# A hybrid decoder layer on one core: part of the weight-splitting work of the recurrent stage goes to GpSimd, with the steps around it rearranged

## The chip, the cores and the metric

The kernel runs on one core of a Trainium2 chip. The metric is device time in microseconds for one execution. An execution is profiled by the hardware on top of the timed runs.

## What is computed

One inference step of one layer, for a prompt of 256 tokens and 8 sequences that decode one token each: 264 columns in all, model width 2048.

```
x = x + 0.5 * swiglu(rmsnorm(x, n1), f1g, f1u, f1d)      # d_ff 5504
proj = rmsnorm(x, nm) @ w_in                             # q, k, v and the RWKV columns
o_att  = sliding-window attention with sinks and relative bias (prompt and decode)
o_rwkv = RWKV-7 time mixing:  S = S*exp(lw) + (S @ -kk)(kk*a)^T + v k^T ;  y = S @ r
x = x + concat(o_att, o_rwkv) @ w_out
x = x + 0.5 * swiglu(rmsnorm(x, n2), f2g, f2u, f2d)
y = rmsnorm(x, final)
```

Beside y, the key and value windows, the recurrent state and the shift state are returned. In the time mixing, `kx = k * (1 + (a - 1) * ka)`.

## The kernel before, in words

Activations lie with features on the partitions and the 264 columns along the free dimension. All weights come from memory once, as chunks of up to 128 x 512 (four 128 x 128 blocks). A chunk is split in `chunk`: SyncE loads `raw`, ScalarE rounds it to `hi` (line 123), and `lo = raw - hi` is subtracted by the engine passed as `e` (through the helper `tt`, line 58). `gemm` multiplies each block three times: hi by the activations' upper part, hi by their lower part, lo by the upper part. There are 6 `raw` buffers and 4 each of `hi` and `lo`. In `gemm` the engine for `lo` is VectorE, always. The buffers are taken with high priority, so that chunks are prepared ahead.

The program has three stages. The first feed-forward ends at about 754 us, with the first chunk load of w_in. The recurrent stage (`mixing_body`) runs to about 1250 us, the second feed-forward to the end. Only the recurrent stage is edited.

In the recurrent stage the weight stream is w_in, 38 tiles of 4 chunks (`win`): two small tiles, then three tiles for each of 8 pairs of RWKV heads, then 4 key and value tiles, then 8 query tiles. w_out follows in three passes over its 16 outputs (`PASS`): pass 0 takes the mixed tiles 0 to 3 (one chunk an output), pass 1 the tiles 8 to 11, 4 and 5, pass 2 the tiles 6, 7 and 12 to 15 (each one full and one half chunk an output). Mixed tiles 0 to 7 are RWKV pairs, 8 to 15 attention tiles.

The rest of the stage is written as generators (tasks). After each chunk, `tick` gives every live task one turn. Tasks are:

- `prep`, one for each pair: decays, keys, the products for the chunked recurrence, and the copies of the 8 decode columns into `XD` by GpSimd.
- `chain`, one for each batch of two pairs (four batches, 0 to 3). It inverts unit triangular 32 x 32 blocks by forward substitution: 30 steps `s`, each a multiply into `st` and an add into `Xt` on VectorE, with a turn's end after every `NSTEP` steps. The result goes to memory (`sb<-Xt`) and comes back transposed over partitions (`TT<-sb`), with `DWAIT` turns of pause ahead of the substitution and behind the transfer; the identity is added to TT; then come VectorE transposes (`TN`), products on TensorE, copies into `W` and `uv`, a three-step scan over chunks, the group norm (`gnorm`, its reciprocal in line 677) and the gate product (`m<-sgl,ld`).
- `attend`, one for each query tile, and `dec_attend`, one for each four query tiles: scores, `softmax`, transposes, probabilities times V (for decode: `m<-uv,bk`), and for decode another transpose (line 818) and a copy into the query tile's last columns.

`drain` gives turns to the tasks whose results a pass needs before the pass is written; `split` then makes upper and lower parts of the mixed tiles, lower ones on GpSimd and VectorE in turn. The order of instructions within each engine is set when the program is built, by a scheduler that simulates times and follows the priorities. Each engine works its queue in order.

Of the kernel before, what the change touches and what calls it, by code (L numbers as in the profile page):

```python
# [9 lines left out]
AF = mybir.ActivationFunctionType  # L10
ALU = mybir.AluOpType
AX = mybir.AxisListType

P = 128
# [7 lines left out]
NPAIR = 8  # L22
NSH = 26
NIN = 38
HALF = (slice(0, 64), slice(64, 128))
# [4 lines left out]
NS, NO, NY, NH, NT, NLD = 38, 8, 8, 40, 18, 6  # L30
NWARM = 14
NGM, NKR, NUV, NTT, NBT = 10, 5, 3, 2, 5
NSTEP = 4
DWAIT = (8,8,8,4)
PW = (2, 1, 3, 2, 2)
ALPHA = math.exp(-0.5)
LKV = 26
# [5 lines left out]
VMU, VKK, VKA, VA0, VRK, VLW, VLB, VSK, VSD = 64, 90, 98, 106, 114, 122, 130, 138, 154  # L43
# [4 lines left out]
def body(tc, I, O):  # L48
    nc = tc.nc
    V, A, G, TE, SP = nc.vector, nc.scalar, nc.gpsimd, nc.tensor, nc.sync  # L50
# [6 lines left out]
    def tt(e, out, a, b, op):  # L57
        return e.tensor_tensor(out=out, in0=a, in1=b, op=op)  # L58
# [4 lines left out]
    def ts(e, out, a, s1, op0, s2=None, op1=None):  # L63
        k = {} if op1 is None else dict(op1=op1)
        e.tensor_scalar(out=out, in0=a, scalar1=s1, scalar2=s2, op0=op0, **k)

    def act(out, in_, f, **k):
        return A.activation(out=out, in_=in_, func=f, **k)  # L68

    def bc(ap, shape):  # L70
        return ap.broadcast_to(list(shape))
# [23 lines left out]
    with ExitStack() as ctx:  # L95
# [20 lines left out]
        def chunk(src, n, e, ahead=True):  # L116
            w = n * P
            with tc.high_priority() if ahead else nullcontext():
                raw = wp.tile([P, CH * P], F32, tag="raw", bufs=NRAW, name=uid("raw"))
                hi = wp.tile([P, CH * P], F32R, tag="hi", bufs=NHL, name=uid("hi"))  # L120
                lo = wp.tile([P, CH * P], F32R, tag="lo", bufs=NHL, name=uid("lo"))
                SP.dma_start(raw[:, :w], src)  # L122
                A.copy(hi[:, :w], raw[:, :w])  # L123
                tt(e, lo[:, :w], raw[:, :w], hi[:, :w].bitcast(F32), ALU.subtract)
            return hi, lo

        def gemm(ps, src, xs, step=None, rng=None, ahead=True):
            n = len(xs)
            for k0 in range(0, n, CH):
                k1 = min(n, k0 + CH)  # L130
                if rng and k0 not in rng:
                    continue
                hi, lo = chunk(src[:, k0 * P:k1 * P], k1 - k0, V, ahead)
                for k in range(k0, k1):
                    xh, xl = xs[k]
                    c = slice((k - k0) * P, (k - k0 + 1) * P)
                    mm(ps[:, :T], hi[:, c], xh, k == 0, False)
                    mm(ps[:, :T], hi[:, c], xl, False, False)
                    mm(ps[:, :T], lo[:, c], xh, False, k == n - 1)
                if step:  # L140
                    step()

        vec = cp.tile([P, NVEC], F32, name="vec")
# [13 lines left out]
        def vc(i):  # L157
            return vec[:, i:i + 1]
# [173 lines left out]
        def mixing_body(mx, n2, n3, XD):  # L332
            def fix(shape, name):
                return mx.tile(list(shape), F32, name=name)
# [9 lines left out]
            ident, bo, cm = C[:, CID:CID + P], C[:, CBO:CBO + P], C[:, CCM:CCM + P]  # L344
# [8 lines left out]
                G.memset(pj[:, 0:1], 0.0)  # L353
            nmu = fix((P, NSH), "nmu")
            mu = vec[:, VMU:VMU + NSH]
            ts(V, nmu, mu, -1.0, ALU.mult, 1.0, ALU.add)
            tt(V, ss, ss, bc(mu.unsqueeze(2), (P, NSH, NB)), ALU.mult)
            nbat = len(BATCH)
# [2 lines left out]
            mixed = [None] * 16  # L361
            have = [False]

            def win(t):
                ps = acc()
                gemm(ps, I["win"][t], n2.xs, tick)
                if not have[0]:
                    n2.rstd(rs)
                    have[0] = True
                return ps  # L370
# [20 lines left out]
            def prep(p, bt, k, xrr, xk, xv):  # L391
# [7 lines left out]
                sg, a = tmp(), tmp()  # L399
# [20 lines left out]
                rk = tmp((P, T + 2 * NB))  # L420
                stt(b, b, 1e24, kk, ALU.min, ALU.mult)
                tt(V, b, b, a, ALU.mult)
                ts(V, a, a, 1.0, ALU.subtract, vc(VKA + p), ALU.mult)
                kx = a
                stt(kx, a, 1.0, xk, ALU.add, ALU.mult)
                stt(rk[:, :T], xrr, vc(VRK + p), kx, ALU.mult, ALU.mult)
# [43 lines left out]
                for h in range(2):  # L470
# [3 lines left out]
                    for blk in range(2):  # L474
                        x = blk * 32
# [12 lines left out]
                for c in range(4):  # L488
                    for h in range(2):
                        r, o = HALF[h], HALF[1 - h]  # L490
# [24 lines left out]
            def chain(bt):  # L515
                n = bt.n
                while bt.left:
                    yield
                nr = n * 16
                ng = P // nr  # L520
                if ng == 3:
                    ng = 2
                nj = 32 // ng
                X = ring((ng * nr, 32, 32), "X", 1)
                Y = ring((ng * nr, nj, 32), "Xt", 1)
# [8 lines left out]
                for s in range(1, 31):  # L534
# [5 lines left out]
                    if s % NSTEP == 0:  # L540
                        yield
                for g in range(ng):
                    SP.dma_start(scr2[bt.i].rearrange("r (j g t) -> g r j t", g=ng, t=32)[g], Y[g * nr:(g + 1) * nr])
                yield from pause(1)
                for h in range(2):
# [2 lines left out]
                        SP.dma_start(TT[x:x + 32, :, blk * 32:blk * 32 + 32],  # L548
                                     scr2[bt.i].rearrange("(h b m) (s t) -> h b s m t", h=2, b=2, s=32)[h, blk])
                yield from pause(DWAIT[bt.i])  # L550
                for h in range(2):
                    for blk in range(2):
                        x = h * 64 + blk * 32
                        v = TT[x:x + 32, :, blk * 32:blk * 32 + 32]
                        tt(V, v, v, bc(ident[x:x + 32, x:x + 32].unsqueeze(1), (32, n * 4, 32)), ALU.add)
                TN = ring((P, n * 4, 32), "TN", 1)
                for h in range(2):
                    V.transpose(TN[h * 64:h * 64 + 32], TT[h * 64:h * 64 + 32, :, 0:32])
# [32 lines left out]
                for k in range(n):  # L591
                    v = wus[k].rearrange("p (c t) -> p c t", c=4)
                    A.copy(W[:, k], v[:, 1:4, 0:64])
                    for h in range(2):
                        V.tensor_copy(uv[HALF[h], :, k, HALF[h]], v[HALF[h], :, 64:128])  # L595
                yield
                pbs = [mp() for _ in range(n)]
                for k in range(n):
# [104 lines left out]
            def softmax(s, mxv, sinks, n):  # L703
                nm, sm, es = (ring((P, 2), "st" + x, 6) for x in "abc")
                ts(V, nm[:, :n], mxv[:, :n], -1.0, ALU.mult)
                for j in range(n):
                    act(s[j], s[j], AF.Exp, bias=nm[:, j:j + 1], accum_out=sm[:, j:j + 1])
                act(es[:, :n], nm[:, :n], AF.Exp, bias=sinks)
                tt(V, sm[:, :n], sm[:, :n], es[:, :n], ALU.add)
                V.reciprocal(sm[:, :n], sm[:, :n])  # L710
                for j in range(n):
                    ts(V, s[j], s[j], sm[:, j:j + 1], ALU.mult)

            def attend(t, q):
                p = t // 4
# [162 lines left out]
            for pi, ks in enumerate(PASS):  # L878
                now = need(ks)
                drain(now, [g for g in tasks if g not in now])  # L880
                with tc.high_priority():
                    for k in ks:
                        split(k)
                for o in range(KD):
                    ps = acc()
                    gemm(ps, I["wout"][o, :, k0 * P:(k0 + len(ks)) * P], [mixed[k] for k in ks], tick)
                    with tc.high_priority():
                        tt(V, xr[o], ps[:, :T], xr[o], ALU.add)
                    if pi == len(PASS) - 1 and o < CH:
                        n3.split(xr[o], tag="y")  # L890
                for k in ks:
                    mixed[k] = None
                k0 += len(ks)
# [148 lines left out]
```

## Time and profile before

| | |
|---|---|
| median of 3 runs | 2026.01 us (2024.55 to 2027.55) |
| profiled execution | 2027.84 us, its span 2026.1 us |
| mean granted TensorE clock | 0.994 |
| recurrent stage, about 770 to 1215 us | 445 us, VectorE busy 339 us, ScalarE 258 us, GpSimd 51 us |

In the rows, PE is TensorE's matmuls, PEld its weight loads, DVE VectorE, ACT ScalarE, POOL GpSimd, SP SyncE. A group's row has line, engine, operation, output<-inputs by the program's names, shapes, count, then busy us and mean ns of one, then idle time of the engine just ahead and what ended it. In the chain of waits, a row is start, length and what the end of the program depended on.

### The profile page before, as it was taken

What the parts mean: (1) busy time and instruction counts of PE and PEld (TensorE: products, weight loads), DVE (VectorE), ACT (ScalarE), POOL (GpSimd) and SP (SyncE); (2) the same over time, 40 slices, a digit from 0 to 9 for tenths busy, and PEclk for the clock granted to TensorE, in tenths of its full rate; (3) what the DMA queues carried; (4) which work ended last, traced back from release to release, by engine and by line L of the source; (5) the groups of instructions that cost most, each with busy time, mean ns of one, the idle gap of its engine ahead of it and who ended that gap; (6) DMA issues with size and microseconds to landing.
All of it is one profiled execution on the core that took longest, in us unless ns stands there. A gap on an engine that the chain in (4) does not pass through costs nothing.

```text
span 2026.1 us, 45592 instructions
## 1 busy us (share of the span) xinstructions
PE 1994.1 (98%) x17126; PEld 1956.0 (97%) x17126; DVE 1324.4 (65%) x2674; ACT 1041.4 (51%) x2054; POOL 240.8 (12%) x342
## 2 busy tenths in 40 slices
PE   9999999999999999999999899999999999999998
PEld 9999999999999999998888789999999999999998
DVE  5865555655556577678778766775666666566665
ACT  5644444444444466665454555554444444444445
POOL 0401001010110122111110000120101101010012
PEclk9999999999999999999999999999999999999999
DMA  6565565655556566554456335565565555655654
GB/s 228 177 187 196 183 192 189 186 184 177 185 171 191 181 205 205 154 157 124 141 148 174 117 102 188 172 185 176 191 182 194 180 191 190 187 191 180 197 180 144
DMA packets 228798, 358.73 MB, mean 177 GB/s; under 512 B 42568, under 2 KB 83680, under 8 KB 228576
## 3 DMA queue, kind: packets, MB, share of 16 engines
q1 hardware_dynamic: 222112, 347.28, 54.6%
q10 hardware_dynamic: 6464, 8.54, 1.3%
q8 instruction: 134, 2.20, 0.4%
q14 instruction: 88, 0.72, 0.1%
HBM read 347.58 MB, written 10.22 MB: 177 GB/s over the span
## 4 chain that ended last, share of the span: by engine, by line
PE 94%; DVE 2%; DMA 2%; ACT 1%; SPq 1%; issue 1%; ACTq 0%; DVEq 0%
PE acc L74 85%; PE m L74 8%; DVE lo L58 1%; DMA TT<-sb 0%; DMA sb<-Xt 0%; DVE y L58 0%; DMA raw<-in_gu 0%; DMA ld<-in_sT 0%; DVE st L58 0%; SPq L122 0%; DVE Xt L58 0%; ACT t L68 0%; DVE uv L595 0%; DMA Xt<-sa 0%; PE m L495 0%
## 5 line engine op out<-in xcount | busy, mean ns | idle before, releaser
L58 DVE TENSOR_TENSOR lo<-raw,hi 128x512 fp32r<-128x512 f32 (+2 forms) x1304 | 871.8, 673 | 552.5 <-ACT hi L123 526.5
L123 ACT CAST hi<-raw 128x512 fp32r<-128x512 f32 (+2 forms) x1304 | 779.3, 602 | 861.6 <-PE acc L74 776.3
L74 PE MATMUL acc<-s,hi 128*128 128x264 f32 x5940 | 1107.3, 286 | 3.9 <-DVE s L58 1.6
L74 PEld LDWEIGHTS acc<-s,hi 128*128 128x128 f32 x5940 | 922.9, 188 | 10.0 <-ACT hi L123 2.2
L74 PE MATMUL acc<-s,lo 128*128 128x264 f32 x2970 | 848.3, 286 | 4.4 <-DVE lo L58 4.4
L74 PEld LDWEIGHTS acc<-s,lo 128*128 128x128 f32 x2970 | 559.5, 189 | 9.1 <-DVE lo L58 5.6
L74 PE MATMUL acc<-t,hi 128*128 128x264 f32 x2752 | 503.1, 284 | 0.0
L74 PEld LDWEIGHTS acc<-t,hi 128*128 128x128 f32 x2752 | 426.4, 188 | 0.0
L74 PE MATMUL acc<-t,lo 128*128 128x264 f32 x1376 | 389.0, 285 | 0.0
L58 POOL TENSOR_TENSOR t<-t,t 128x264 f32<-128x264 f32 (+1 forms) x148 | 150.7, 1018 | 1150.6 <-ACT hi L123 790.4
L74 PEld LDWEIGHTS acc<-t,lo 128*128 128x128 f32 x1376 | 258.4, 188 | 0.1
L74 PE MATMUL acc<-y,hi 128*128 128x264 f32 x648 | 124.5, 284 | 0.0
L74 PEld LDWEIGHTS acc<-y,hi 128*128 128x128 f32 x648 | 101.3, 188 | 0.2
L74 PE MATMUL acc<-y,lo 128*128 128x264 f32 x324 | 92.2, 285 | 0.0
L58 DVE TENSOR_TENSOR t<-acc,t 128x264 f32<-128x264 f32 x156 | 67.4, 432 | 36.8 <-PE acc L74 36.5
L58 POOL TENSOR_TENSOR o<-o,o 128x264 f32<-128x264 f32 x43 | 36.4, 846 | 222.7 <-ACT o L68 217.8
L74 PE MATMUL acc<-o,hi 128*128 128x264 f32 x324 | 62.8, 284 | 0.0
L74 PEld LDWEIGHTS acc<-y,lo 128*128 128x128 f32 x324 | 60.7, 187 | 0.0
L61 DVE SCALAR_TENSOR_TENSOR s<-acc,s 128x264 f32<-128x264 f32 x96 | 40.5, 427 | 16.0 <-PE acc L74 15.5
L74 PEld LDWEIGHTS acc<-o,hi 128*128 128x128 f32 x324 | 50.0, 188 | 0.0
L74 PE MATMUL m<-s,hi 128*128 128x264 f32 x260 | 48.5, 285 | 0.0
L61 DVE SCALAR_TENSOR_TENSOR x<-acc,x 128x264 f32<-128x264 f32 x96 | 40.5, 426 | 10.1 <-PE acc L74 9.6
(234 smaller groups left out, 1295.9 us busy)
## 6 DMA issues: line engine op xcount, KB each, us to landing
raw<-in_gu SPq DMA_DIRECT2D x688, 256.0 KB, 3.3
raw<-in_dn SPq DMA_DIRECT2D x224, 256.0 KB, 2.7
raw<-in_win SPq DMA_DIRECT2D x152, 256.0 KB, 3.5
raw<-in_dn SPq DMA_DIRECT2D x160, 192.0 KB, 2.7
raw<-in_wout SPq DMA_DIRECT2D x48, 256.0 KB, 3.3
raw<-in_wout SPq DMA_DIRECT2D x32, 128.0 KB, 2.9
xsp<-x ACTq DMA_DIRECT2D x16, 132.0 KB, 3.2
s<-xsp SPq DMA_DIRECT2D x16, 132.0 KB, 4.0
```

Of the source, the lines that this page charges most:

```text
L58: return e.tensor_tensor(out=out, in0=a, in1=b, op=op)
L61: return V.scalar_tensor_tensor(out=out, in0=a, scalar=s, in1=b, op0=op0, op1=op1)
L74: TE.matmul(out, lhsT, rhs, start=start, stop=stop, **k)
L123: A.copy(hi[:, :w], raw[:, :w])
```

## The change

`gemm` gets an argument `share` and a counter of chunks over the whole kernel; a chunk whose number is a multiple of `share` has its `lo` subtracted by GpSimd. `win` passes 3 for the first 30 tiles and 2 for the query tiles, the output projection 2. The rest of the edits: the substitution ends a turn after 2 steps instead of 4, and the last batch's pauses go from 4 to 8 turns; the identity is no longer added to TT by VectorE but set into the diagonal of Xt by GpSimd before the transfer; `(a-1)*ka` becomes one ScalarE instruction with a precomputed `-ka`; half of the uv copy and one of two softmax scales go to ScalarE, the other scale to GpSimd.

```diff
-NSTEP = 4
-DWAIT = (8,8,8,4)
+NSTEP = 2
+DWAIT = (8, 8, 8, 8)
...
+        nch = [0]
+
-        def gemm(ps, src, xs, step=None, rng=None, ahead=True):
+        def gemm(ps, src, xs, step=None, rng=None, ahead=True, share=0):
...
-                hi, lo = chunk(src[:, k0 * P:k1 * P], k1 - k0, V, ahead)
+                nch[0] += 1
+                hi, lo = chunk(src[:, k0 * P:k1 * P], k1 - k0, G if share and nch[0] % share == 0 else V, ahead)
...
+            nka = fix((P, NPAIR), "nka")
+            ts(G, nka, vec[:, VKA:VKA + NPAIR], -1.0, ALU.mult)
...
-                gemm(ps, I["win"][t], n2.xs, tick)
+                gemm(ps, I["win"][t], n2.xs, tick, share=2 if t >= LKV + 4 else 3)
...
-                ts(V, a, a, 1.0, ALU.subtract, vc(VKA + p), ALU.mult)
+                act(a, a, AF.Identity, scale=vc(VKA + p), bias=nka[:, p:p + 1])
...
                 for g in range(ng):
+                    d = Y[g * nr:(g + 1) * nr].rearrange("p j t -> p (j t)")
+                    G.memset(d[:, g:nj * 32:32 + ng], 1.0)
+                for g in range(ng):
                     SP.dma_start(scr2[bt.i]..., Y[g * nr:(g + 1) * nr])
...
-                for h in range(2):
-                    for blk in range(2):
-                        x = h * 64 + blk * 32
-                        v = TT[x:x + 32, :, blk * 32:blk * 32 + 32]
-                        tt(V, v, v, bc(ident[x:x + 32, x:x + 32].unsqueeze(1), (32, n * 4, 32)), ALU.add)
...
-                    for h in range(2):
-                        V.tensor_copy(uv[HALF[h], :, k, HALF[h]], v[HALF[h], :, 64:128])
+                    V.tensor_copy(uv[HALF[0], :, k, HALF[0]], v[HALF[0], :, 64:128])
+                    A.copy(uv[HALF[1], :, k, HALF[1]], v[HALF[1], :, 64:128])
...
-                for j in range(n):
-                    ts(V, s[j], s[j], sm[:, j:j + 1], ALU.mult)
+                ts(G, s[0], s[0], sm[:, 0:1], ALU.mult)
+                A.mul(s[1], s[1], sm[:, 1:2])
...
-                    gemm(ps, I["wout"][o, :, k0 * P:(k0 + len(ks)) * P], [mixed[k] for k in ks], tick)
+                    gemm(ps, I["wout"][o, :, k0 * P:(k0 + len(ks)) * P], [mixed[k] for k in ks], tick, share=2)
```

GpSimd's queue in the middle of the w_in tiles, before: `shc` and `XD` are the small copies, `wc` a copy of the decays, t_... its sources.

```order
L436 COPY XD<-t_11766 128x8
L414 MEMSET t_11812 128x4
L418 COPY wc<-t_11812 128x4
L58 TENSOR_TENSOR XD<-XD 128x8
L377 COPY shc<-pj_10574 128x9
L436 COPY XD<-t_11767 128x8
L436 COPY XD<-t_11763 128x8
```

and at such a place in the changed kernel:

```order
L58 TENSOR_TENSOR XD<-XD 128x8
L58 TENSOR_TENSOR lo_11555<-raw_11553,hi_11554 128x512
L382 COPY shc<-pj_10574 128x9
L441 COPY XD<-t_11392 128x8
L58 TENSOR_TENSOR lo_11658<-raw_11656,hi_11657 128x512
L441 COPY XD<-t_11388 128x8
L382 COPY shc<-pj_10572 128x9
```

A subtraction stands between the small copies every few rows; the copies themselves are the same.

## The prediction

> **What bounds the kernel now.** The page comes first: one engine is full.
>
> ```profile
> span 2026.1 us, 45592 instructions
> PE 1994.1 (98%) x17126; PEld 1956.0 (97%) x17126; DVE 1324.4 (65%) x2674; ACT 1041.4 (51%) x2054; POOL 240.8 (12%) x342
> ```
>
> TensorE has the span, so only what TensorE waits for can move the time. The table of stretches says where it waits: columns are busy time of PE, PEld, DVE, ACT, POOL with instruction counts, then the granted clock, DMA share and GB/s. The first row is a stretch of the first feed-forward for comparison; the rest is the recurrent stage.
>
> ```profile
> 650.00:700.00 50.00, 50.00 (x415) 50.00 (x413) 27.29 (x44) 24.48 (x43) 8.68 (x8) 1.00 0.52 181
> 770.00:850.00 80.00, 80.00 (x716) 77.38 (x714) 54.63 (x101) 57.47 (x124) 13.83 (x41) 1.00 0.59 179
> 850.00:900.00 50.00, 49.10 (x468) 46.66 (x467) 43.20 (x130) 30.84 (x76) 11.47 (x22) 1.00 0.53 148
> 900.00:950.00 50.00, 47.65 (x556) 44.58 (x555) 42.15 (x125) 25.81 (x60) 5.43 (x16) 0.97 0.45 129
> 950.00:1000.00 50.00, 45.91 (x535) 42.82 (x534) 32.77 (x79) 29.78 (x68) 6.10 (x19) 0.97 0.51 145
> 1000.00:1050.00 50.00, 47.92 (x450) 45.26 (x448) 42.99 (x127) 28.68 (x65) 4.73 (x15) 1.00 0.47 134
> 1050.00:1100.00 50.00, 48.55 (x588) 44.40 (x586) 36.77 (x114) 22.74 (x52) 2.51 (x6) 1.00 0.58 168
> 1100.00:1150.00 50.00, 46.51 (x556) 39.85 (x554) 41.42 (x151) 26.92 (x81) 1.44 (x2) 1.00 0.53 161
> 1150.00:1200.00 50.00, 44.45 (x300) 35.14 (x301) 35.17 (x127) 27.20 (x85) 5.63 (x17) 0.86 0.27 78
> 770.00:1215.00 445.00, 425.10 (x4278) 389.59 (x4277) 339.13 (x977) 258.47 (x634) 51.14 (x138) 0.98 0.50 145
> ```
>
> The feed-forward stretch has no idle PE, and 50 us over 415 matmuls give 120.5 ns each, 1.45 us for a chunk of 12. From 850 to 1200 PE is idle for 0.90 + 2.35 + 4.09 + 2.08 + 1.45 + 3.49 + 5.55 = 19.9 us. The clock adds (0.03 + 0.03 + 0.14) x 50 = 10.0 us of lost full speed, all of it in stretches with long idle time. So 29.9 us can be won at most: 13.9 before 1100 (10.9 idle, 3.0 clock) and 16.0 behind it (9.0 and 7.0). The last row is the whole stage: VectorE is busy for 339.13 of 445 us (76%), GpSimd for 51.14, ScalarE for 258.47.
>
> Whom PE waits for (total, times, longest):
>
> ```profile
> PE acc L74 <- DVE lo L58: 4.4, 5, 1.5
> PE m L74 <- DVE uv L595: 3.7, 5, 1.9
> PE m L805 <- DVE bk L65: 3.2, 1, 3.2
> ```
>
> It is VectorE nearly each time, and the two longest parts are things the change edits. The chain of waits shows the worst place, the end of pass 0 of the output projection:
>
> ```profile
> 1144.98 0.67 PE m L74 x29
> ...
> 1151.87 0.30 DVE bk L65
> ...
> 1153.54 1.88 DVE t L677 x2
> 1155.41 1.51 issue
> ...
> 1161.41 0.44 PE m L818 x2
> ...
> 1165.08 0.81 PE acc L74 x2
> ```
>
> Pass 1 needs the first decode attention. Its scores are made at 1144.98 and its result lets the projection go on at 1165.08. In between its softmax scale (L65) is late, and then two reciprocals of batch 3's group norm (L677) stand in VectorE's queue ahead of its next step.
>
> **The change part by part.** Durations, from the stage's groups on VectorE, ScalarE and GpSimd (busy, mean ns; then idle time ahead of them):
>
> ```profile
> L58 DVE TENSOR_TENSOR lo<-raw,hi 128x512 fp32r<-128x512 f32 x179 | 121.8, 685 | 44.6 <-ACT hi L123 37.0 <-PE acc L74 6.3
> L58 DVE TENSOR_TENSOR lo<-raw,hi 128x256 fp32r<-128x256 f32 x15 | 6.2, 415 | 0.2 <-ACT hi L123 0.2
> L595 DVE COPY uv<-m 64x256 f32<-64x256 f32 x16 | 6.7, 421 | 0.3
> L58 DVE TENSOR_TENSOR TT<-TT,C 32x256 f32<-32x256 f32 x16 | 6.7, 417 | 12.8 <-DMA TT<-sb 12.5
> L65 DVE TENSOR_SCALAR t<-t,stb 128x256 f32<-128x256 f32 x16 | 6.1, 381 | 0.3
> L65 DVE TENSOR_SCALAR t<-t,stb 128x128 f32<-128x128 f32 x16 | 4.5, 279 | 0.0
> L65 DVE TENSOR_SCALAR t<-t,vec 128x264 f32<-128x264 f32 x8 | 2.8, 350 | 0.0
> L68 ACT ACTIVATE t<-t,vec 128x264 f32<-128x264 f32 x8 | 4.1, 513 | 0.0
> L58 DVE TENSOR_TENSOR st<-X,Xt 128x60 f32<-128x60 f32 x16 | 3.4, 216 | 0.3
> L58 POOL TENSOR_TENSOR s<-y,s 128x264 fp32r<-128x264 f32 x4 | 2.9, 744 | 41.3 <-PE m L74 40.0 <-ACT s L870 1.3
> L58 POOL TENSOR_TENSOR XD<-XD 128x8 f32<-128x8 f32 x8 | 1.6, 204 | 1.7 <-ACT XD L68 1.6
> ```
>
> *Lower parts to GpSimd.* The chunk counter runs through the whole kernel and stands at 536 when the stage starts (344 gate/up and 192 down chunks). Of the 120 chunks of the first 30 tiles every third goes over: 40. Of the 32 of the query tiles every second: 16. Pass 0 has 16 chunks: 8. In passes 1 and 2 each output takes a full chunk and a half one, so "every second" always falls on the half one: 32 half chunks. VectorE loses 64 x 0.685 + 32 x 0.415 = 57.1 us. No row has a GpSimd subtraction of 512 columns. From 8 columns (204 ns) to 264 (744 ns) it is 2.11 ns a column, so 744 + 248 x 2.11 = 1.27 us, and 0.73 us for 256. GpSimd takes 64 x 1.27 + 32 x 0.73 = 104.7 us more.
>
> *Other moves off VectorE.* The 16 identity additions on TT, 6.7 us. The uv copy's second half, 8 x 0.421 = 3.4. The line (a-1)*ka, 2.8. The softmax scales, 6.1 + 4.5, and about 1 for the decode ones. With the 57.1, 81.6 us leave VectorE. GpSimd gets 18 wide scales, near its 744 ns row, 13 us, and 16 small memsets, about 2: some 119 us in all. ScalarE gets 8 x 0.513 for the a line and some 0.3 us for each of 8 uv copies and 18 scales, about 12 us. At 258 of 445 us busy that is hidden behind its waits for PE, and costs at most 12 where it is not.
>
> The wait for TT stays: VectorE stood 12.5 us before the additions, and the first reader is now the transpose, in the same in-order queue with weight chunks behind it. The diagonal's memsets add GpSimd to the chain before the transfer. I book nothing for either; a VectorE queue with fewer rows ahead of the transpose could stand there longer, by up to the 12.5 us over again.
>
> *NSTEP 4 to 2, DWAIT 8.* A task's turn in the substitution has 4 VectorE instructions of about 0.2 us instead of 8, so a weight chunk's subtraction queues behind 0.9 us and not 1.7. The chain takes 15 turns instead of 7, and batch 3 waits 2 x 4 longer. At 1.45 us a turn that is 12 us per batch, 23 us for batch 3. Batch 3 is needed for pass 2 only, 16 + 32 chunks behind the query tiles, which covers it; the first decode attention waits for batch 2 alone. Uncovered it would cost those 12 us.
>
> What all this does to the worst place shows in TensorE's order. Before, the eight uv,bk rows (first decode attention, probabilities times V) and its last transposes (m<-C,t) come after pass 0's last matmul, and pass 1 (acc_16984) follows:
>
> ```order
> L74 MATMUL acc_16940<-s_16485,lo_16943 128x264
> ...
> L74 MATMUL m_16033<-uv_15298,bk_15911 32x128 x8
> ...
> L74 MATMUL m_16085<-sgl,ld_15950 128x264
> L74 MATMUL m_16089<-sgl,ld_15952 128x264
> ...
> L818 MATMUL m_16101<-C,t_16042 128x128 x2
> ...
> L74 MATMUL acc_16984<-s_16960,hi_16986 128x264
> ```
>
> In the changed kernel they come after the last query tile (acc_16079), ahead of pass 0 (acc_16399):
>
> ```order
> L74 MATMUL acc_16079<-s_10551,lo_16262 128x264
> L74 MATMUL m_15826<-uv_15552,bk_15728 32x128 x8
> ...
> L821 MATMUL m_15886<-C,t_15835 128x128 x2
> L74 MATMUL m_15929<-t_15822,s_14742 64x256
> L74 MATMUL m_15929<-t_15882,s_14742 64x256
> L74 MATMUL m_15929<-t_15823,s_14742 64x128
> L74 MATMUL m_15929<-t_15883,s_14742 64x128
> L74 MATMUL acc_16399<-s_16383,hi_16401 128x264
> ```
>
> They moved up by a whole pass, and batch 3's norm (m<-sgl) is no longer among them. VectorE's rows ahead of the step that follows (t<-bk,bk,m), before:
>
> ```order
> L65 TENSOR_SCALAR bk_15911<-bk_15911,stb_15916 128x129 x2
> L677 RECIPROCAL t_15956<-t_15956 128x264
> L677 RECIPROCAL t_15960<-t_15960 128x264
> L745 COPY t_16030<-m_16025 128x128
> L58 TENSOR_TENSOR y_15584<-m_15954,t_15956 128x264
> L61 SCALAR_TENSOR_TENSOR t_16042<-bk_15299,bk_15911,m_16033 128x128 x2
> ```
>
> and now:
>
> ```order
> L713 RECIPROCAL stb_15733<-stb_15733 128x2
> L58 TENSOR_TENSOR lo_16402<-raw_16400,hi_16401 128x512
> L58 TENSOR_TENSOR lo_16506<-raw_16504,hi_16505 128x512
> L748 COPY t_15823<-m_15818 128x128
> L61 SCALAR_TENSOR_TENSOR o_16349<-acc_16079,rs 128x264
> L61 SCALAR_TENSOR_TENSOR t_15835<-bk_15553,bk_15728,m_15826 128x128 x2
> ```
>
> The 264-wide reciprocals (1.88 us of the chain, and 1.51 us of "issue" behind them) are gone from the way. The stop does not vanish: pass 0's first inputs are now split on GpSimd behind the copies of this attention's result. I give it 2 us (ScalarE copy, four GpSimd copies and a 0.74 us split, less the attention matmuls beside them).
>
> *The price on VectorE.* Where both engines read SBUF, the trace shows them taking turns. These are VectorE and GpSimd rows of the second feed-forward (start, us), twice the same VectorE instruction:
>
> ```profile
> 1424.58 0.93 POOL L58 TENSOR_TENSOR t<-t,t 128x264 fp32r<-128x264 f32 x1 [0.91 <-ACT t L264]
> 1424.81 0.97 DVE L58 TENSOR_TENSOR sd<-sd,sd 128x256 f32<-128x256 f32 x1
> 1426.31 0.41 DVE L58 TENSOR_TENSOR sd<-sd,sd 128x256 f32<-128x256 f32 x1
> ```
>
> Beside a GpSimd subtraction it takes 0.97 us, alone 0.41. The Trainium skill says this as a rule against the change: in "SBUF — State Buffer", section "Who interferes with whom", a VectorE instruction with two SBUF inputs and a GpSimd instruction that reads SBUF exclude each other for the whole instruction. The trace agrees in these rows; the rule taken strictly gives the upper bound below.
>
> The weight subtraction has two SBUF inputs, as have most steps of prep and the substitution. So the 119 us of new GpSimd work block VectorE for between 0 and 119 us. VectorE is busy 76% of the time and runs into such an instruction halfway through on average: 119 x 0.76 x 0.5 = 45 us. VectorE's work changes by -82 + 45 = -37 us (from -82 to +37), from 339 to some 302.
>
> **The sum.** Behind 1100: 16.0 us to be had, of which I take 12, less 2 for the new stop: -10. Before 1100: 13.9 to be had; with a tenth less VectorE work and shorter bursts I take a third, 5, and give 2 back for subtractions that come late from GpSimd, whose queue is in order and holds copies that wait for VectorE: -3. Together -13 us on the profiled execution's 2027.84, 2014.8. The median of the runs stands 1.83 lower, so 2013.0. A measurement of this kernel can tell about 0.2%, 4 us, from no change.
>
> **The rivals.**
>
> *All of it is won.* For: nothing but waits is lost in the stage. Against: 37 us of relief is a ninth, and the TT waits stay. 2026 - 30 = 1996. Chance 0.14.
>
> *The stop only moves.* The decode attention ends at the end of the query tiles with the same gap as before, since its own steps are in series (1144.98 to 1165.08). For: PE has little else in those rows. Against: the two reciprocals are out of the way. Only the 3 us before 1100 are left, give or take 4: 2023. Chance 0.14, half of it faster by over 4 us, half within.
>
> *GpSimd and VectorE in each other's way: slower.* Each moved subtraction holds VectorE's next one up by half its length, and one that waits its turn reaches PE late. 64 x 0.64 + 32 x 0.36 = 52 us of delay. It decides once more than a quarter of it (13 of 52) reaches PE. At 40%, 21 - 13 = 8 us slower, 2034; all of it would give 2065. For: the rows above, and VectorE 43 of 50 us busy in the worst stretches. Against: four hi and lo buffers let a subtraction finish up to three chunks, 4.35 us, ahead of its use. The strict form of this is the Trainium skill's rule in the section named above. Chance 0.22.
>
> *It does less than it says* is in the forecast already: in passes 1 and 2 only half chunks move.
>
> **How the numbers follow.** Forecast 0.50, with its own range of 2004 to 2020. Faster: 0.50 + 0.14 + 0.07 = 0.71; the same 0.07; slower 0.22. The range reaches to both outer cases' values, 1996 and 2034, and leaves their far halves out.
>
> **What would show it.** Right: PE idle and lost clock between 1100 and 1200 fall from 16 to about 6 us, the uv,bk matmuls of the first attention come before the first in_wout matmul, VectorE's time in the stage near 300 us, GpSimd's near 170 with a 128x512 lo of 1.3 to 2 us. Wrong: PE waiting for POOL lo by more than 13 us in all, or DVE lo means of 0.9 us or more, or a stop of over 8 us at the end of the query tiles.

## The result and the profile after

The changed kernel takes 2020.92 us in the median of 16 runs (2018.12 to 2024.23) beside 2027.78 us for the kernel before (16 runs). The ratio is 0.9967, with an interval of 0.9959 to 0.9974: 6.9 us faster, about half of the 13 us forecast. The profiled execution took 2023.6 us, 2.7 above its median, so its own gain on the profiled execution of before is 4.2 us.

The page's first lines for the changed kernel:

```profile
span 2021.8 us, 45680 instructions
PE 1986.9 (98%) x17126; PEld 1953.9 (97%) x17126; DVE 1288.0 (64%) x2510; ACT 1054.1 (52%) x2089; POOL 364.8 (18%) x473
```

Over the whole program VectorE went from 1324.4 to 1288.0 us, that is -36.4 where the prediction said -37. GpSimd gained 124 us. The total of the relief came as forecast. The table of stretches shows that it did not turn into time where it was expected to:

```profile
770.00:850.00 80.00, 78.90 (x708) 76.35 (x707) 49.41 (x84) 55.77 (x123) 31.30 (x57) 1.00 0.59 178
850.00:900.00 50.00, 47.31 (x434) 44.28 (x432) 42.72 (x117) 30.52 (x75) 19.14 (x34) 0.97 0.50 140
900.00:950.00 50.00, 44.22 (x524) 40.99 (x524) 34.64 (x112) 26.97 (x64) 14.19 (x27) 0.90 0.45 118
950.00:1000.00 50.00, 48.05 (x490) 44.98 (x489) 37.58 (x86) 32.25 (x78) 15.80 (x28) 1.00 0.54 148
1000.00:1050.00 50.00, 46.81 (x528) 43.19 (x528) 36.58 (x98) 28.49 (x68) 11.40 (x21) 1.00 0.47 126
1050.00:1100.00 50.00, 44.48 (x529) 40.81 (x528) 32.67 (x124) 26.06 (x69) 17.64 (x25) 1.00 0.53 143
1100.00:1150.00 50.00, 47.85 (x435) 40.68 (x435) 32.07 (x110) 34.77 (x103) 27.01 (x37) 0.97 0.63 194
1150.00:1200.00 50.00, 50.00 (x558) 45.55 (x555) 35.11 (x95) 31.17 (x86) 18.50 (x24) 1.00 0.33 97
770.00:1215.00 445.00, 422.61 (x4313) 391.82 (x4312) 308.44 (x835) 272.95 (x675) 161.96 (x258) 0.98 0.52 147
```

Between 1100 and 1200 PE is idle for 2.15 us and the clock costs 0.03 x 50 = 1.5, together 3.7 where it was 16.0. Between 770 and 1100 the idle time is 1.10 + 2.69 + 5.78 + 1.95 + 3.19 + 5.52 = 20.2 us, and the clock costs (0.03 + 0.10) x 50 = 6.5: 26.7 where it was 13.9. So 12.4 us were won behind 1100 and 12.8 lost ahead of it. By these rows nothing would be gained over 770 to 1200. Over the whole program PE is even idle for longer (34.9 us where it was 32.0), and busy for 7.2 us less (1994.1 to 1986.9) with the same 17126 matmuls: the last row too counts 35 matmuls more than before in 2.5 us less busy time. So the gain lies inside PE's busy time. It may be gaps too short to show as idle (matmul ends are modelled); no row here shows them. From the first w_in load to the last w_out load, the stage shortened by 4.6 us.

Those load rows of SyncE's queue, of before and then of the changed kernel, also show that the same clock time holds different work:

```profile
L122 SPq DMA_DIRECT2D raw<-in_win x152: 327/328/1773, 754.7 to 1078.3; - x152
L122 SPq DMA_DIRECT2D raw<-in_wout x80: 327/328/505, 1083.8 to 1246.1; - x80
```

```profile
L122 SPq DMA_DIRECT2D raw<-in_win x152: 327/328/2142, 756.6 to 1107.8; - x152
L122 SPq DMA_DIRECT2D raw<-in_wout x80: 327/328/1496, 1108.3 to 1243.4; - x80
```

The stretch of w_in, up to the first w_out load, grew from 329.1 to 351.7 us. That of w_out shrank from 162.3 to 135.1. The scheduler moved side work (attention and the recurrent chains) from the out projection to places beside w_in, and the stops went with it. Counted on TensorE from the first product of w_in to that of w_out, 1526 small matmuls (`m`) stood beside w_in before and 1666 now; beside w_out 540, and 400 now. PE's idle time went from 11.7 to 20.2 us beside w_in, and from 8.2 to 2.1 beside w_out.

Whom PE waits for now:

```profile
PE acc L74 <- DVE lo L58: 4.5, 4, 1.8
PE m L74 <- ACT uv L598: 3.9, 2, 3.6
PE m L74 <- ACT W L596: 2.8, 1, 2.8
PE acc L74 <- POOL s L58: 2.1, 1, 2.1
...
PE acc L74 <- POOL lo L58: 1.4, 2, 1.1
```

GpSimd's weight subtractions are hardly waited for (1.4 us), and the stop at the end of the query tiles is there and costs 2.1 us (`POOL s`). The longest wait is new, for `uv`. On TensorE, then in the chain of waits (start, length):

```profile
933.39 0.28 PE L74 MATMUL acc<-s,hi 128*128 128x264 f32 x1
937.30 0.48 PE L74 MATMUL m<-BT,W 64*64 64x64 f32 x4 [3.63 <-ACT uv L598]
```

```profile
935.84 0.21 DVE Xt L58
936.05 0.02 issue
936.08 0.21 DVE st L58
936.29 0.02 issue
936.32 0.20 DVE Xt L58
936.52 0.34 DVE uv L597
936.85 0.02 issue
936.88 0.38 ACT uv L598
937.25 0.04 issue
937.30 5.93 PE m L74 x112
```

The first half of the uv copy waits in VectorE's queue behind substitution steps of another batch (`st`, `Xt`), the second half on ScalarE starts when it has ended, and TensorE stands for 3.63 us, since the next weight matmuls come later in its order.

### The profile page after: what moved, and what is told of

Its sections match the earlier page's. It is cut to its first block, busy times and chain, and to the rows that moved or that the text cites. A ratio compares the mean times of both kernels' runs of the same rounds, so it can differ in the third digit from the quotient of the medians.

```text
span 2021.8 us, 45680 instructions
## 1 busy us (share of the span) xinstructions
PE 1986.9 (98%) x17126; PEld 1953.9 (97%) x17126; DVE 1288.0 (64%) x2510; ACT 1054.1 (52%) x2089; POOL 364.8 (18%) x473
## 3 DMA queue, kind: packets, MB, share of 16 engines
q1 hardware_dynamic: 222112, 347.28, 57.1%
## 4 chain that ended last, share of the span: by engine, by line
PE 91%; DVE 4%; DMA 2%; issue 1%; ACT 1%; SPq 1%; POOL 0%; ACTq 0%; DVEq 0%; POOLq 0%
PE acc L74 83%; PE m L74 7%; DVE st L58 1%; DVE lo L58 1%; DVE Xt L58 1%; DMA raw<-in_win 1%; DVE t L61 0%; DMA sa<-gm 0%; POOL lo L58 0%; DMA raw<-in_gu 0%; DMA sb<-Xt 0%; DMA Xt<-sa 0%; DVE y L58 0%; DMA X<-sa 0%; ACT t L68 0%
## 5 line engine op out<-in xcount | busy, mean ns | idle before, releaser
L58 DVE TENSOR_TENSOR lo<-raw,hi 128x512 fp32r<-128x512 f32 (+1 forms) x1208 | 819.0, 681 | 562.7 <-ACT hi L123 540.0
L74 PE MATMUL acc<-s,hi 128*128 128x264 f32 x5940 | 1112.9, 286 | 3.8 <-POOL s L58 2.1
L74 PEld LDWEIGHTS acc<-s,hi 128*128 128x128 f32 x5940 | 925.7, 189 | 10.7 <-POOL s L58 2.4
L74 PE MATMUL acc<-s,lo 128*128 128x264 f32 x2970 | 849.6, 286 | 5.9 <-DVE lo L58 4.5
L74 PEld LDWEIGHTS acc<-s,lo 128*128 128x128 f32 x2970 | 560.1, 189 | 9.5 <-DVE lo L58 5.5
L74 PE MATMUL acc<-t,hi 128*128 128x264 f32 x2752 | 503.0, 285 | 0.0
L74 PEld LDWEIGHTS acc<-t,hi 128*128 128x128 f32 x2752 | 426.5, 188 | 0.0
L74 PE MATMUL acc<-t,lo 128*128 128x264 f32 x1376 | 389.1, 285 | 0.0
L74 PEld LDWEIGHTS acc<-t,lo 128*128 128x128 f32 x1376 | 258.5, 188 | 0.1
L58 POOL TENSOR_TENSOR lo<-raw,hi 128x512 fp32r<-128x512 f32 (+1 forms) x96 | 110.3, 1150 | 119.6 <-ACT hi L123 105.6
L74 PE MATMUL acc<-y,hi 128*128 128x264 f32 x648 | 123.9, 285 | 0.0
L74 PEld LDWEIGHTS acc<-y,hi 128*128 128x128 f32 x648 | 101.1, 188 | 0.2
L74 PE MATMUL acc<-y,lo 128*128 128x264 f32 x324 | 92.1, 284 | 0.0
L74 PE MATMUL acc<-o,hi 128*128 128x264 f32 x324 | 62.1, 281 | 0.0
L74 PEld LDWEIGHTS acc<-y,lo 128*128 128x128 f32 x324 | 60.9, 188 | 0.0
L74 PEld LDWEIGHTS acc<-o,hi 128*128 128x128 f32 x324 | 50.0, 188 | 0.0
L74 PE MATMUL m<-s,hi 128*128 128x264 f32 x260 | 49.0, 287 | 0.0
```

What stands on the lines that cost most here:

```text
L74: TE.matmul(out, lhsT, rhs, start=start, stop=stop, **k)
```

## The experiments

The change has three parts: **S**, the share of GpSimd in the subtractions; **N**, the turns (`NSTEP` 2, `DWAIT` 8); **M**, all other moves. Each run is compared with the kernel before on the same chip (medians 2029.9 to 2030.3 us).

**No share** (M + N): S is taken out of the changed kernel.

```diff
-                gemm(ps, I["win"][t], n2.xs, tick, share=2 if t >= LKV + 4 else 3)
+                gemm(ps, I["win"][t], n2.xs, tick)
...
-                    gemm(ps, I["wout"][o, ...], [mixed[k] for k in ks], tick, share=2)
+                    gemm(ps, I["wout"][o, ...], [mixed[k] for k in ks], tick)
```

> The changed kernel with every lower part back on VectorE (share left out), all other edits kept. Theory T (the stop): the change gains by moving the first decode attention ahead of pass 0, about 12 us, and loses about as much again in the middle of the stage because the side work that used to pile up at the stop is now interleaved earlier with its own waits; without the share the attention still stands ahead of pass 0 in TensorE's order, so the time stays near the changed kernel's 2021, 2019 to 2025, with VectorE some 15 to 20 us busier. Theory G (GpSimd in the way): the middle's loss comes from GpSimd's subtractions being late and locking VectorE out; without them the stop stays gone and the middle recovers, 2010 to 2016. Theory N (turns): the loss comes from the shorter, more numerous turns; no change, 2020 to 2022.

Measured: 0.9919 (0.9905 to 0.9933), 2013.8 us, in the range of theory G. Without the share, the kernel is faster by another 4.8 thousandths, 10 us.

**The share alone** (S): on the kernel before, only `nch` and `share`, with the arguments of the changed kernel.

```diff
...
+                nch[0] += 1
-                hi, lo = chunk(src[:, k0 * P:k1 * P], k1 - k0, V, ahead)
+                hi, lo = chunk(src[:, k0 * P:k1 * P], k1 - k0, G if share and nch[0] % share == 0 else V, ahead)
...
```

> The kernel before with the share alone. T: the attention's last step stands some 5 chunks ahead of pass 1 in the order, so most of the stop goes and the middle loses little: 2017 to 2023. G: slower than before or no better, 2027 to 2035. N: without the new turns the share's relief is whole, 2013 to 2017.

Measured: 0.9967 (0.9955 to 0.9979), 2023.22 us. No theory's range holds it; that of T is nearest. The same edit that costs 10 us in the changed kernel wins 7 here.

**The old turns** (S + M): on the changed kernel,

```diff
-NSTEP = 2
-DWAIT = (8, 8, 8, 8)
+NSTEP = 4
+DWAIT = (8,8,8,4)
```

> The changed kernel with NSTEP 4 and DWAIT (8,8,8,4) again, share and the other moves kept. T: the attention stands 5 chunks ahead of pass 1, so the stop is nearly gone and the time is near the changed kernel's, 2018 to 2023. N: the middle's loss goes, 2010 to 2016. G: no change, 2020 to 2023.

Measured: 0.9916 (0.9904 to 0.9929), 2012.95 us. Theory N's range holds it, and G, which held for the run without share, has missed.

**The new turns alone** (N): the same two lines the other way, on the kernel before.

```diff
-NSTEP = 4
-DWAIT = (8,8,8,4)
+NSTEP = 2
+DWAIT = (8, 8, 8, 8)
```

> The kernel before with NSTEP 2 and DWAIT 8 alone. T: the order puts the first decode attention right behind the start of pass 0, so the stop goes, but VectorE has all its old work: 2020 to 2026. G: the stop goes and the middle has no GpSimd work, 2012 to 2017. N: slower than before, 2028 to 2035.

Measured: 0.9972 (0.9963 to 0.998), 2024.01 us, in the range of theory T. So no theory held throughout. Each of S and N helps when alone, and each hurts where the other is. The next two runs complete the table.

**The other moves alone** (M): the changed kernel with the edits of "no share" and of "the old turns" together.

```diff
+NSTEP = 4
+DWAIT = (8,8,8,4)
...
+                gemm(ps, I["win"][t], n2.xs, tick)
...
```

> Only the other moves (identity by memset, the a line, uv copies, softmax scales); no share, NSTEP 4 and DWAIT (8,8,8,4). On a scale where before is 2030. Theory A (parts add): the stalls of the first half of the stage come from the share (about 6 us) and those of the second half from the short turns (about 10), so without both the time is 2003 to 2010. Theory B (one stop to be had once): each of the share, the turns and the moves pulls the first decode attention ahead, and only that pays; here its last step stands half a chunk ahead of pass 1, so a good part of the stop is back: 2013 to 2022.

Measured: 0.9947 (0.993 to 0.9965), 2018.94 us, in the range of theory B; the parts do not add.

**Share and turns without the moves** (S + N): on the kernel before, the edits of "the share alone" and "the new turns alone".

```diff
+NSTEP = 2
+DWAIT = (8, 8, 8, 8)
...
+                hi, lo = chunk(src[:, k0 * P:k1 * P], k1 - k0, G if share and nch[0] % share == 0 else V, ahead)
...
```

> Share and new turns, without the other moves; TensorE's order is nearly that of the changed kernel, so this prices the moves at equal order. Before is 2030, the changed kernel would be 2023. If VectorE's load sets the middle (24 us more of it): 2027 to 2033. If the order alone sets it: 2021 to 2025.

Measured: 1.003 (1.002 to 1.0041), 2036.18 us, slower than before and above both ranges. All eight combinations, as the change of the ratio in thousandths:

| | long turns (4) | short turns (2) | what N does |
|---|---|---|---|
| nothing else | 0 | -2.8 | -2.8 |
| S | -3.3 | +3.0 | +6.3 |
| M | -5.3 | -8.1 | -2.8 |
| S + M | -8.4 | -3.3 | +5.1 |

M is worth -5.1 to -6.3 in every pairing. S is worth -3.3 and -3.1 at long turns, and +5.8 and +4.8 at short ones. The clash of S and N is 3.0 + 3.3 + 2.8 = 9.1 without M, and -3.3 + 8.4 + 8.1 - 5.3 = 7.9 with it. Intervals added as independent make that 9.1 +- 1.8 and 7.9 +- 2.7, or 18 and 16 us. N is always both settings here, `NSTEP` and the last batch's pause; which of them clashes, these runs do not tell. One row each of the stretch 770 to 1215 for M + N, S + M, M, and S + N:

```profile
770.00:1215.00 445.00, 428.22 (x4382) 395.75 (x4382) 327.83 (x927) 278.57 (x686) 79.36 (x179) 0.99 0.53 149
```

```profile
770.00:1215.00 445.00, 432.64 (x4402) 401.20 (x4402) 321.86 (x850) 278.75 (x689) 163.62 (x263) 0.99 0.54 151
```

```profile
770.00:1215.00 445.00, 428.89 (x4376) 397.46 (x4375) 327.65 (x925) 278.01 (x684) 74.74 (x179) 0.99 0.54 149
```

```profile
770.00:1215.00 445.00, 414.39 (x4214) 382.40 (x4213) 328.33 (x892) 254.94 (x630) 138.87 (x217) 0.97 0.52 141
```

Idle plus lost clock (1 less the clock, times 445) are 16.8 + 4.5 = 21.2, 12.4 + 4.5 = 16.8, 16.1 + 4.5 = 20.6 and 30.6 + 13.4 = 44.0 us. In the changed kernel they are 22.4 + 8.9 = 31.3. S + M, at nearly the same GpSimd time over the whole program (362.9 us for 364.8) and more VectorE time (1293.6 for 1288.0) than the changed kernel, stops for 10 us less: the load on the engines alone does not set the time. The whole-program times of VectorE say the same. The share frees 7.7 us of it alone (1324.4 to 1316.7), 10.7 beside N, 12.1 beside M and 17.0 beside both: it frees least where it wins 7 us, and most where it costs 10.

**Zeros instead of subtractions.** GpSimd writes twice into `lo` without reading. The lower parts of GpSimd's chunks are so left out of the result. This takes away the reading of SBUF, and also GpSimd's wait for `raw` and `hi`.

```diff
-                tt(e, lo[:, :w], raw[:, :w], hi[:, :w].bitcast(F32), ALU.subtract)
+                if e is G:
+                    for _ in range(2):
+                        G.memset(lo[:, :w].bitcast(F32), 0.0)
+                else:
+                    tt(e, lo[:, :w], raw[:, :w], hi[:, :w].bitcast(F32), ALU.subtract)
```

> The changed kernel, but where GpSimd would subtract it writes zeros twice over the same tile: the lower parts of those chunks are left out. GpSimd is busy about as long and reads nothing, and TensorE's order is nearly the same. Changed kernel: 2023 on this scale. If GpSimd's reads lock VectorE out and that costs the middle: VectorE's time in the stage falls from 308 to about 270 and the time to 2010 to 2017. If GpSimd's late results cost it: 2015 to 2020, VectorE's time unchanged. If neither: 2021 to 2025.

Measured: 0.9912 (0.9892 to 0.9932), 2011.42 us, in the first range; VectorE's time in the stage fell to 288.9 us, half of the way to the 270 expected. The page's engine line, the row of the stage, and two groups of this kernel:

```profile
PE 1981.3 (99%) x17126; PEld 1946.9 (97%) x17126; DVE 1259.2 (63%) x2510; ACT 1052.9 (52%) x2089; POOL 339.2 (17%) x569
```

```profile
770.00:1215.00 445.00, 428.37 (x4393) 396.32 (x4392) 288.94 (x847) 278.63 (x687) 141.56 (x341) 1.00 0.54 150
```

```profile
L61 DVE SCALAR_TENSOR_TENSOR t<-t,vec,t 128x264 f32<-128x264 f32 x8 | 4.0, 495 | 0.1
L126 POOL MEMSET lo<- 128x512 f32 x124 | 65.1, 526 | 85.0 <-PE acc L74 81.9
```

VectorE has the same 2510 instructions as in the changed kernel and 28.8 us less to do. The same group and others in the changed kernel, and the first one in the kernel before:

```profile
L58 POOL TENSOR_TENSOR lo<-raw,hi 128x512 fp32r<-128x512 f32 x62 | 82.2, 1327 | 74.0 <-ACT hi L123 67.9 <-ACT t L747 2.9 <-DMA Xt<-sa 1.7
L58 POOL TENSOR_TENSOR lo<-raw,hi 128x256 fp32r<-128x256 f32 x16 | 12.6, 791 | 23.1 <-ACT hi L123 16.7 <-ACT t L747 2.6 <-PE acc L74 2.4
L61 DVE SCALAR_TENSOR_TENSOR t<-t,vec,t 128x264 f32<-128x264 f32 x8 | 7.9, 990 | 0.1
```

```profile
L61 DVE SCALAR_TENSOR_TENSOR t<-t,vec,t 128x264 f32<-128x264 f32 x8 | 3.9, 484 | 0.0
```

An instruction of 484 ns takes 990 beside the subtractions and 495 beside writes. This group is the most marked one, and its mean depends on what the order puts beside it: 720 ns in S + M, 535 in S + N. Of the 120 steps `st<-X,Xt` the longest took 234 ns before and 1331 in the changed kernel. A single case in the changed kernel's timeline, GpSimd and then VectorE:

```profile
877.61 1.29 POOL L58 TENSOR_TENSOR lo<-raw,hi 128x512 fp32r<-128x512 f32 x1 [1.16 <-ACT hi L123]
```

```profile
877.40 0.23 DVE L58 TENSOR_TENSOR Xt<-Xt,st 128x70 f32<-128x70 f32 x1
877.67 1.31 DVE L58 TENSOR_TENSOR st<-X,Xt 128x65 f32<-128x65 f32 x1
879.02 0.23 DVE L58 TENSOR_TENSOR Xt<-Xt,st 128x65 f32<-128x65 f32 x1
```

A substitution step of some 0.23 us is held until the GpSimd subtraction is over. The Trainium skill's rule in "SBUF — State Buffer", section "Who interferes with whom", that a VectorE instruction with two SBUF inputs contends with GpSimd reading SBUF and not with GpSimd only writing, agrees with these rows.

**The uv copy back on VectorE.** On the changed kernel:

```diff
-                    V.tensor_copy(uv[HALF[0], :, k, HALF[0]], v[HALF[0], :, 64:128])
-                    A.copy(uv[HALF[1], :, k, HALF[1]], v[HALF[1], :, 64:128])
+                    for h in range(2):
+                        V.tensor_copy(uv[HALF[h], :, k, HALF[h]], v[HALF[h], :, 64:128])
```

> The changed kernel with both halves of the uv copy on VectorE again; TensorE's order is nearly the same. In the changed kernel the ScalarE half starts when the VectorE half has ended, and TensorE waits 3.9 us for it. If that split costs: 2018 to 2021 against 2023. If the wait is VectorE's queue ahead of both: 2022 to 2025.

Measured: 0.9973 (0.9963 to 0.9983), 2024.21 us, in the second range. No gain, and the stop for `uv` stays (`PE m L74 <- DVE uv L598: 2.9, 1, 2.9`), so splitting the copy did not make it; the rows above put it down to VectorE's queue ahead of the copy.

**Where the clash is.** Two runs keep the short turns and share only late, or only early. Late (query tiles and out projection):

```diff
-                gemm(ps, I["win"][t], n2.xs, tick, share=2 if t >= LKV + 4 else 3)
+                gemm(ps, I["win"][t], n2.xs, tick, share=2 if t >= LKV + 4 else 0)
```

> The changed kernel with the share for the query tiles and the output projection alone; none in the first 30 tiles. On a scale where before is 2030, the changed kernel 2023 and the one without share 2014. If the conflict of share and short turns sits where prep and the substitution run (two-input steps on VectorE): 2008 to 2014. If it sits in the attention part or at the end of the query tiles: 2019 to 2024.

Measured: 0.9916 (0.9902 to 0.9931), 2013.19 us, in the first range.

Early (the first 30 tiles alone):

```diff
-                gemm(ps, I["win"][t], n2.xs, tick, share=2 if t >= LKV + 4 else 3)
+                gemm(ps, I["win"][t], n2.xs, tick, share=0 if t >= LKV + 4 else 3)
...
-                    gemm(ps, I["wout"][o, ...], [mixed[k] for k in ks], tick, share=2)
+                    gemm(ps, I["wout"][o, ...], [mixed[k] for k in ks], tick)
```

> The reverse: every third chunk of the first 30 tiles to GpSimd, none behind them; TensorE's order up to the query tiles is that of the changed kernel. Conflict in prep and substitution: 2021 to 2026. Conflict behind them: 2012 to 2017.

Measured: 0.9959 (0.9944 to 0.9974), 2022.18 us, again the range for prep and substitution. The loss is with the early share, beside prep and the substitution; the late share costs nothing. The stage's row of the late share, with 16.3 us idle and a full clock:

```profile
770.00:1215.00 445.00, 428.74 (x4401) 396.49 (x4400) 323.90 (x886) 279.77 (x689) 123.84 (x224) 1.00 0.54 150
```

**Late share at long turns**: S + M ("the old turns") without the early share.

```diff
+NSTEP = 4
+DWAIT = (8,8,8,4)
...
+                gemm(ps, I["win"][t], n2.xs, tick, share=2 if t >= LKV + 4 else 0)
```

> As the first of these, with NSTEP 4 and DWAIT (8,8,8,4): the moves and the late share. The moves alone gave 2019, the moves with the whole share 2013. If the late share relieves the stretch around the stop: 2010 to 2015. If it is the early share that paid there: 2016 to 2020.

Measured: 0.9958 (0.9941 to 0.9975), 2021.44 us, above both ranges. At long turns the early share is worth 4.2 thousandths, 8.5 us (0.9958 to 0.9916); at short turns it costs 5.1, 10 us (0.9916 to 0.9967).

**Turns of three steps.** On the changed kernel:

```diff
-NSTEP = 2
-DWAIT = (8, 8, 8, 8)
+NSTEP = 3
+DWAIT = (8,8,8,4)
```

> The changed kernel with NSTEP 3 and DWAIT (8,8,8,4): whole share, all moves. TensorE's order lies between that of NSTEP 2 (2023) and NSTEP 4 (2013). If the conflict grows with how early the order puts the side work: 2014 to 2020. If it is the short turn itself: 2011 to 2014.

Measured: 1.0034 (1.0021 to 1.0047), 2037.82 us. Both ranges missed: the value between the two is worse than either, 25 us from turns of four steps with the same pauses. Its stage:

```profile
770.00:1215.00 445.00, 422.19 (x4204) 388.05 (x4204) 306.96 (x824) 264.46 (x662) 155.22 (x251) 0.96 0.51 141
```

Idle time is that of the changed kernel (22.8 and 22.4 us), while the clock is 0.96 for 0.98: 17.8 us of lost speed for 8.9. That is some 9 of the 13.6 us (6.7 thousandths) by which it is behind the changed kernel, as far as two digits of the clock tell. Its longest stop is one of 5.7 us for `TT` (`PE m L74 <- ACT TT L582: 5.7, 1, 5.7`).

The expectation took its order for one between the other two, and it is not. Counted in the traces as above, with the time from the first product of w_in to the first of w_out, and from there to the second feed-forward:

| | beside w_in | small matmuls there | beside w_out | small matmuls there |
|---|---|---|---|---|
| before | 338.3 us | 1526 | 153.7 us | 540 |
| changed kernel | 363.6 us | 1666 | 123.8 us | 400 |
| old turns (S + M) | 346.5 us | 1623 | 129.9 us | 443 |
| zeros | 354.8 us | 1666 | 123.0 us | 400 |
| three steps | 386.2 us | 1928 | 114.3 us | 138 |

The order of three steps puts side work furthest ahead of all. The kernel with zeros has the changed kernel's split, and its small matmuls stand in the mean 0.46 of a weight chunk (12 weight matmuls) from their places there (2.2 in the run without share). So at nearly the same order, what GpSimd's subtractions do beyond writing costs 8.8 us beside w_in and 0.8 beside w_out.

## Where the prediction was right and where it failed

*VectorE's relief: right in total, by luck.* It was -36.4 us for -37, over the whole program. The price of GpSimd's subtractions was close: 1327 and 791 ns for 1.27 and 0.73 us. Within the relief, though, the terms were off. Without the share VectorE's engine line is this:

```profile
PE 1984.2 (99%) x17126; PEld 1949.6 (97%) x17126; DVE 1305.0 (65%) x2606; ACT 1054.1 (52%) x2089; POOL 266.8 (13%) x377
```

So M and N together took off 19.4 us (24.5 were booked for the moves), and the share's 57.1 us of moved work took off 17.0. With zeros in place of the subtractions it would take off 45.8 (1305.0 to 1259.2), and the blocking, put at 45, takes back 28.8 of that. Two reliefs 5 and 11 us too high and a price 16 too high cancel. Work moved to GpSimd freed under a third of its VectorE time here, and a seventh of it where the share stands alone (7.7).

*Behind 1100, -10: right by the rows.* It measured 12.4 us less idle and lost clock. The first decode attention went ahead of pass 0 and the new stop measured 2.1 us for the 2 given. All that the prediction named as signs of being right came (3.7 us left between 1100 and 1200 for about 6, VectorE 308 us in the stage, GpSimd 162, `lo` at 1.33 us), and none of the signs of being wrong. They watched the end of the stage and TensorE's direct waits, and the loss came elsewhere.

*Before 1100, -3: the step that failed.* It measured +12.8 by the same rows. The prediction took a tenth less VectorE work and shorter bursts as a cause of shorter waits, each by itself, in an order taken as given. The runs showed three things in its place. First, the order is rebuilt: work that used to sit beside w_out now sits beside w_in (22.6 us more there by the loads, 140 small matmuls), with its stops. Second, the bursts did not get shorter. In the order of VectorE's timeline the longest string of substitution instructions with nothing between them is 11 before (2.8 us) and 14 in the changed kernel (4.3 us); of all 240, 18% stood in strings of more than four before, 45% after, and 27% with the new turns alone. A turn's end lets other work come between, and the scheduler need not put any there. Third, the share and the short turns, which help by 7 and 6 us alone, clash by 16 to 18 us together, in the early tiles. The strings alone are not the clash: in S + M 45% stand in long ones too.

*The rival of engines in each other's way: its mechanism ran, its place was wrong.* PE waited 1.4 us for GpSimd's `lo`, not 13. The blocking shows in VectorE's own short steps instead. With the blocking and GpSimd's waits taken away, the share at short turns costs nothing: 0.9912 for the zeros beside 0.9919 for no share. Since that run has nearly the changed kernel's order, the order alone does not make the loss: the clash needs GpSimd's reading or its waits. The run took away both, and does not tell one from the other; that PE waited for GpSimd's `lo` for 1.4 us in all speaks for the reading, and does not show it.

*What M is worth* was the part least worked out: 24.5 us of moves with no gain booked of their own. M alone gives 11 us, of 13 forecast for the whole change.

*Open:* which rows carry the clash. With long turns the same share slows the same steps and there is no loss: the 240 substitution instructions take 48.6 us before, 58.2 in the changed kernel and 61.7 in S + M. So it is not the sum of the blocking but how it meets an order that the scheduler built. Which places of the order make the difference is not shown, nor which of `NSTEP` and `DWAIT` does (three steps with the old pauses lose too), nor which of the moves in M gains.

The best versions here are the old turns with share and moves (0.9916), the late share at short turns (0.9916) and no share (0.9919). Their intervals overlap.

## What to carry to other kernels

Moving subtractions with two SBUF inputs to GpSimd freed VectorE of far less than their duration here (8 to 17 of 57 us), while the other moves freed 18.7 of the 24.5 us booked (1324.4 to 1305.7); so price the blocking first. Where a scheduler sets the order, a relief of an engine that is not the bound is a licence to repack and not a gain: split such a change into its parts and run them in all combinations, since two edits that win 6 to 7 us each lost 6 together. Count what stands beside each phase of the work, and not only what a stretch of clock time holds, when the order may move work from one phase to another. And set a sign of being wrong for every term of a sum: the term ahead of 1100 had none of its own here.

## What was not expected of the hardware

The granted clock fell after some short stops and not after others as long or longer. In the changed kernel's timeline TensorE stands once for 1.43 us, and the fine table of stretches shows a half clock for 3.4 us, from 1.7 us behind the end of the stop:

```profile
872.51 0.33 PE L74 MATMUL m<-uv,gm 64*64 64x64 f32 x2 [1.43 <-DVE gm L58]
```

```profile
867.40:874.20 6.80, 5.37 (x57) 4.73 (x54) 6.56 (x23) 2.30 (x7) 1.65 (x1) 1.00 0.57 161
874.20:877.60 3.40, 3.40 (x16) 3.33 (x16) 3.19 (x13) 2.56 (x7) 0.91 (x2) 0.50 0.50 133
877.60:884.00 6.40, 6.40 (x52) 6.28 (x51) 5.60 (x15) 6.32 (x12) 1.96 (x5) 1.00 0.41 114
```

With the old turns (S + M), at the same kind of wait, a stop about as long was followed by full clock:

```profile
869.85 0.33 PE L74 MATMUL m<-uv,gm 64*64 64x64 f32 x2 [1.45 <-DVE gm L58]
```

```profile
868.00:880.00 12.00, 10.37 (x89) 9.52 (x88) 10.93 (x39) 8.13 (x15) 2.49 (x5) 1.00 0.42 117
```

In the changed kernel itself a stop of 2.84 us, which ended at 1070.05, was followed by full clock too (the row from 1050 to 1100 has 1.00). In the stop of 3.63 us from 933.67 the half clock began at 935.6 and held for 6.8 us:

```profile
935.60:942.40 6.80, 5.10 (x92) 4.99 (x94) 4.11 (x19) 4.52 (x14) 1.51 (x5) 0.50 0.21 48
```

A short stop can so cost 1.7 us more than itself (half of 3.4), or nothing more: its length alone does not decide. The Trainium skill, "TensorE: Matmul & The Clock Gate", section "Part 1: The HAM clock gate", gives a window of 3413 ns and names at least one idle window as the condition for the lower clock. The 3.4 us of the rows agree with that window; the half clock behind a stop of 1.43 us does not agree with that condition, and the measurement decides.
